# Latents and rotary key projected before the last two gated pairs, from unscaled products

## The chip, the cores and the metric

The kernel runs on one core of a Trainium2 chip. The metric is the device time of one execution in microseconds (us); the median of three runs of the kernel before is 1034.42 us. The engines are TensorE (PE; its weight loads appear as PEld), VectorE (DVE), ScalarE (ACT), GpSimd (POOL) and the queues that issue DMA transfers (SP for nearly all of them). Each engine works through a queue of its own in order; a wait at the head of a queue holds up everything behind it.

## The reference, cut to what matters

Two decoder layers over 512 tokens of 1024 channels, all in float32. Layer 0 normalises its input by rows (RMS norm) and multiplies it by one matrix `w_in`, whose 1696 columns are split:

```python
h = rmsnorm(x, norm_mix_e)                    # x / sqrt(mean(x^2) + EPS) * gain
proj = h @ w_in
a, g = proj[..., :512], proj[..., 512:1024]
u = a * sigmoid(g)                            # gated convolution branch
u = silu(layernorm(causal_dwconv(u, conv_w, conv_b)))   # 31 taps per channel
cq, ckv, kr = proj[..., 1024:1408], proj[..., 1408:1664], proj[..., 1664:]
q  = rmsnorm(cq, q_norm_g) @ w_uq             # 8 heads, 64 plain + 32 rotary columns
kv = rmsnorm(ckv, kv_norm_g) @ w_ukv          # keys and values of 8 heads
# causal attention, then concat([u, o]) @ w_out, residual; gated MLP
```

`cq` and `ckv` are the latents of the attention, `kr` is one rotary key that all heads share. Layer 1 is a pooling mixer and a second gated MLP. The change touches layer 0's mixer alone.

## The kernel before

Channels lie on the partitions and tokens along the free dimension, 512 to a tile. Every weight and every left operand is kept as the sum of two parts, `hi` and `lo`, and each 128x128x512 product is three matmuls (`mm3`, L107 to L109). A weight chunk arrives by DMA as `raw`, ACT copies it to `hi` (L96), DVE subtracts to get `lo` (L97), one chunk ahead of its use, in the order of the list `stream`.

The rows of `x` are multiplied by the norm's gain and projected before the norm's root is known. Its per-token factor `rows0` is applied to the products. `project` (L340s) makes one tile of 128 output columns: 24 matmuls from one `w_in` chunk. The first eight chunks carry four tiles at once (two gated pairs, `acc4`). `w_in1` has ten more chunks: four for the third and fourth gated pair, three for `cq`, two for `ckv`, one for the rotary key. They are projected in that order.

`glu` turns a pair of products into a tile `u` of the convolution: a product with `rows0`, a sigmoid on ACT, another product with `rows0`, one with the other half. Each `u` is convolved in the background. Some taps run on POOL (12, 12, 12 and 16 of the four tiles; L385 multiplies, L387 adds to `side`), one on ACT, the rest on DVE as multiply-adds into a PSUM tile `conv` (L367). A closing addition (L390) joins the two sums; the tiles' DVE taps follow one another. `pump(n, m)` puts the next n DVE taps and m POOL taps into the program.

`latent` projects `cq` or `ckv`: DVE multiplies the product by `rows0` into `t` (L447), ACT makes `hi` of `t` times the latent norm's gain (L101), DVE makes `lo` (L102), ACT squares `t` (L211) and DVE adds the squares (L213). After the key product, `rstd` sums the squares over channels on PE (L225), adds EPS (L229) and takes the inverse root in nine small DVE steps after two for the start value (L192 to L199). The result scales scores, values and keys; for the keys it is spread over partitions by four diagonals on DVE (L240) and products on PE (L241).

For each head, `scores` computes four row blocks. DVE adds the mask and takes the row maximum (L506), scales it by the query factor (L510), ACT takes the exponential (L514); a reciprocal (L520) and four ACT copies (L522) normalise. PE transposes one head behind (L536) and multiplies by the values two heads behind (L548). Queries (L492) are made two heads ahead, keys (L479) per pair of heads. The layer norm's transposes (L614) come when the last head and the convolution are done.

The framework fixes the order of each engine's queue when the program is built, from the traced program and estimates of its own, so instructions can stand in another order than in the code. `behind` keeps conv taps from filling in between the root's steps.

Of the kernel before, what the change touches and what calls it, by code (L numbers as in the profile page):

```python
# [44 lines left out]
def kernel(  # L45
# [71 lines left out]
    def rows_of(t, a, b):  # L117
        return t[a:b, 0, :], t[a:b, 1, :]

# [1 line left out]
    stream = (  # L121
        [(w_in0[k], 512) for k in range(KD)]
        + [(w_in1[m], 1024) for m in range(10)]
# [60 lines left out]
    held = []  # L184

    def behind(i):
        """Background work traced from here on starts after instruction i."""
        held[:] = [i]
# [14 lines left out]
    class Squares:  # L203
        """Sums of squares over the channels: tiles are added up, the last one apart."""
# [12 lines left out]
    def rstd(stats, blocks=range(4)):  # L217
        ps = aux()
        nb = len(blocks)
        v = small(nb * len(stats))  # L220
        for k, st in enumerate(stats):
            for i, b in enumerate(blocks):
                at = 2 * (nb * k + i)
                for n, t in enumerate(st.parts):
                    pe.matmul(  # L225
                        ps[:, at : at + 2], t[:, b * P : (b + 1) * P], ones[:, 0:2],
                        start=n == 0, stop=n == len(st.parts) - 1,
                    )
            dve.tensor_scalar(  # L229
                v[:, nb * k : nb * (k + 1)], ps[:, 2 * nb * k : 2 * nb * (k + 1) : 2],  # L230
                1.0 / st.n, EPS, op0=ALU.mult, op1=ALU.add,
            )
        return rsqrt(v, nb * len(stats))

    def spread_bank(r, blocks=2, tag="aux"):
        """Per-token column to rows: every partition gets the token's value."""
        ps = aux(tag)
        for i in range(blocks):
            d = p_t.tile([P, P], F32, tag="diag", bufs=4, name=uid("d"))
            dve.tensor_scalar(d, ident, r[:, i : i + 1], None, op0=ALU.mult)  # L240
            pe.matmul(ps[:, i * P : (i + 1) * P], ones, d, start=True, stop=True)  # L241
        return ps[:, : blocks * P]
# [7 lines left out]
    # ==== layer 0: conv + latent attention ====  # L250
# [22 lines left out]
    # rotary tables: the turn of each angle from exact products with the digits of 1/(2 pi)  # L273
# [54 lines left out]
    with tc.issue_after(opened.ins):  # L328
        for k in range(KD):
            stat.add(x[k])  # L330
    acc4 = [bank() for _ in range(4)]
    for k in range(KD):
        w = weights(2)
        for m in range(4):
            mm3(acc4[m], part(w, m), pair(xg[k]), k == 0, k == KD - 1)
        if k == 5:
            r0 = rstd([stat])
# [11 lines left out]
    # depthwise conv, in the background: taps on DVE into PSUM, the rest on ACT and Pool  # L349
# [61 lines left out]
    # GLU branch: u = a * sigmoid(g), kept behind CW - 1 zeros  # L411
# [19 lines left out]
    ps_a = project()  # L431
    pump(GLU, 2)
    ps_g = project()
    glu(ps_a, ps_g)
    pump(GLU, 2)
    ps_a = project()
    pump(GLU, 2)
    ps_g = project()
    glu(ps_a, ps_g)
    pump(GLU, 2)  # L440

    def latent(n, gain, width):
        parts, stat = [], Squares(width, dve)
        for m in range(n):
            ps = project()
            t = temp()
            dve.tensor_tensor(t, ps, rows0, op=ALU.mult)  # L447
            parts.append(s4())
            split_scaled(pair(parts[m]), t, c(gain + m))
            stat.add(t)  # L450
            pump(LAT, 2)
        return parts, stat
# [3 lines left out]
    # shared rotary key, replicated over the four row groups  # L456
# [4 lines left out]
    r = rstd([stat_q, stat_kv])  # L461
# [3 lines left out]
    pump(2, 2)  # L465
# [29 lines left out]
    def scores(h):  # L495
# [4 lines left out]
        for i in range(4):  # L500
# [9 lines left out]
            dve.scalar_tensor_tensor(  # L510
                nb[:, i : i + 1], mx[:, i : i + 1], -1.0, q_scale[:, i : i + 1],
                op0=ALU.mult, op1=ALU.mult,
            )
            act.activation(  # L514
                p, p, AF.Exp, bias=nb[:, i : i + 1],
                scale=q_scale[:, i : i + 1], accum_out=ls[:, i : i + 1],
            )
            blocks.append(p)
            pump(BLK, 1)
# [67 lines left out]
    # output projection: attention half first  # L587
# [20 lines left out]
    # layernorm over channels, token-major  # L608
# [42 lines left out]
    def residual(ps, m, gain, scale=None, apart=False):  # L651
        """x[m] += ps (scaled); its parts for the next product, and its squares."""
# [90 lines left out]
    def last_down(gs, ws):  # L743
        """The last channel tile by halves of the tokens, so that the final norm of the
        first half runs beside the products of the second."""
# [20 lines left out]
        def last_rstd():  # L766
            """The second half's columns, by a square root that one step refines."""
# [45 lines left out]
    # ==== layer 1: windowed means, as band matrices over tokens ====  # L813
# [62 lines left out]
def layout(inputs):  # L876
# [8 lines left out]
    def by_col(w):  # L885
        """[K, M] -> [M/128, 128, K/128, 128]: one stationary operand per column tile."""
# [54 lines left out]
    # constants of the shapes  # L941
# [51 lines left out]
```

## Time and profile before

| | |
|---|---|
| median of 3 runs | 1034.42 us (1031.65 to 1035.17) |
| span of the profiled execution | 1028.9 us, first to last instruction |
| busy in the span: PE, PEld, DVE | 989.6 us (96%), 795.5 us (77%), 607.6 us (59%) |
| busy in the span: ACT, POOL | 399.3 us (39%), 189.3 us (18%) |
| time of the profiled execution itself | not given beside the span; the median lies 5.5 us above the span |

Times in the profile count from the start of the span. A group row names line, engine, operation, tiles and shape, then the count, the busy time, the mean of one in ns, and the idle time ahead. A wait row reads: who waited for whom, us in total, times, longest. A queue row has start, duration and the instruction. "PEclk" or "granted clock" is the share of TensorE's full speed that it was given. A matmul's end is modelled, so a long row of matmuls overlaps in the listing.

### The profile page before, as it was taken

To read this page: it belongs to the slowest core of one execution; us is meant where nothing else is said; L and a number is where in the kernel's file an instruction comes from. 1 tells how busy PE (TensorE), PEld (TensorE's weight loads), DVE (VectorE), ACT (ScalarE), POOL (GpSimd) and SP (SyncE) were. 2 spreads that over 40 slices of the span, in tenths; PEclk is the share of its full clock that TensorE was granted. 3 is DMA by queue.
4 is the path that set the end of the run, shared out by engine and by line. 5 is a ranking of instruction groups with operands and counts; after the bars stand their busy time and mean duration, and the time that the engine had idled before them with its cause. 6 is when DMAs were issued, how large, how long until landed. Compare 5 with 4: busy or idle time off the path is not lost.

```text
span 1028.9 us, 11548 instructions
## 1 busy us (share of the span) xinstructions
PE 989.6 (96%) x4444; PEld 795.5 (77%) x4444; DVE 607.6 (59%) x901; ACT 399.3 (39%) x575; POOL 189.3 (18%) x191
## 2 busy tenths in 40 slices
PE   8996698999999999999999999999999999999996
PEld 6885465677888888888888889888888888888886
DVE  6989899958485556565432337585555655522223
ACT  5423277845253333333222235343333333322221
POOL 4399997004000000000001011300000000000101
PEclk9999699999999999999999999999999999999998
DMA  6422101013222222322222242222323222222212
GB/s 194 169 74 72 36 21 62 21 62 103 97 88 89 95 103 82 103 85 100 100 85 103 84 139 75 82 86 100 102 82 103 83 101 86 99 103 82 103 41 82
DMA packets 29479, 91.99 MB, mean 89 GB/s; under 512 B 4081, under 2 KB 6385, under 8 KB 29425
## 3 DMA queue, kind: packets, MB, share of 16 engines
q1 hardware_dynamic: 28880, 90.74, 25.8%
q8 instruction: 34, 0.56, 0.2%
q10 hardware_dynamic: 544, 0.52, 0.1%
q14 instruction: 21, 0.16, 0.1%
HBM read 89.02 MB, written 2.23 MB: 89 GB/s over the span
## 4 chain that ended last, share of the span: by engine, by line
PE 85%; DVE 11%; issue 1%; DMA 1%; ACT 1%; SPq 0%; DVEq 0%
PE ps L109 27%; PE ps L107 27%; PE ps L108 27%; DVE lo L97 2%; DVE conv L367 1%; DVE s L510 1%; DVE prob L506 1%; PE aux L225 1%; DVE xg L102 1%; PE ps L548 1%; PE aux L241 1%; DMA x<-in_xT_dram 0%; DMA col<-in_cols_dram 0%; DVE s L199 0%; DVE s L197 0%
## 5 line engine op out<-in xcount | busy, mean ns | idle before, releaser
L109 PE MATMUL ps<-xg,lo 128*128 128x512 f32 x816 | 323.8, 397 | 4.0 <-DVE lo L97 4.0
L107 PE MATMUL ps<-xg,hi 128*128 128x512 f32 x816 | 325.1, 398 | 2.0 <-ACT hi L96 2.0
L108 PE MATMUL ps<-xg,hi 128*128 128x512 f32 x816 | 324.2, 397 | 0.0
L96 ACT CAST hi<-raw 128x1024 fp32r<-128x1024 f32 (+2 forms) x166 | 169.6, 1024 | 393.3 <-PE ps L108 350.3
L97 DVE TENSOR_TENSOR lo<-raw,hi 128x1024 fp32r<-128x1024 f32 (+2 forms) x166 | 207.2, 1250 | 163.4 <-ACT hi L96 162.8
L109 PEld LDWEIGHTS ps<-xg,lo 128*128 128x128 f32 x816 | 154.0, 189 | 42.9 <-DVE lo L97 5.7
L107 PEld LDWEIGHTS ps<-xg,hi 128*128 128x128 f32 x816 | 154.3, 189 | 39.6 <-ACT hi L96 2.4
L108 PEld LDWEIGHTS ps<-xg,hi 128*128 128x128 f32 x816 | 154.3, 189 | 37.1
L107 PE MATMUL ps<-g,hi 128*128 128x512 f32 (+1 forms) x374 | 143.1, 383 | 0.0
L108 PE MATMUL ps<-g,hi 128*128 128x512 f32 (+1 forms) x374 | 142.9, 382 | 0.0
L109 PE MATMUL ps<-g,lo 128*128 128x512 f32 (+1 forms) x374 | 142.8, 382 | 0.0
L213 POOL TENSOR_TENSOR sqr<-sqr,sqr 128x512 f32<-128x512 f32 x33 | 51.3, 1553 | 322.7 <-ACT sqr L211 321.4
L688 POOL MEMSET t<- 128x2 f32 x44 | 4.3, 99 | 473.0 <-DVE t L702 362.4
L108 PEld LDWEIGHTS ps<-g,hi 128*128 128x128 f32 x374 | 70.4, 188 | 15.0
L107 PEld LDWEIGHTS ps<-g,hi 128*128 128x128 f32 x374 | 70.3, 188 | 15.0
L109 PEld LDWEIGHTS ps<-g,lo 128*128 128x128 f32 x374 | 70.3, 188 | 15.0
L689 DVE TENSOR_TENSOR t<-ps,rows 128x512 f32<-128x512 f32 x44 | 30.4, 690 | 83.8 <-PE ps L109 83.8
L701 DVE TENSOR_TENSOR t<-ps,rows 128x512 f32<-128x512 f32 x44 | 30.4, 690 | 75.0 <-PE ps L109 75.0
L387 POOL TENSOR_TENSOR side<-side,tapped 128x512 f32<-128x512 f32 x48 | 67.8, 1414 | 1.5
L696 DVE SCALAR_TENSOR_TENSOR t<-t,col,t 128x512 f32<-128x512 f32 x88 | 65.6, 748 | 1.4
L385 POOL TENSOR_TENSOR tapped<-u,col 128x512 f32<-128x512 f32 x48 | 59.8, 1267 | 0.0
L699 ACT ACTIVATE t<-t 128x512 f32<-128x512 f32 x44 | 27.8, 631 | 74.4 <-DVE t L696 74.4
(177 smaller groups left out, 935.4 us busy)
## 6 DMA issues: line engine op xcount, KB each, us to landing
raw<-in_w_up_dram SPq DMA_DIRECT2D x88, 512.0 KB, 3.2
raw<-in_w_down_dram SPq DMA_DIRECT2D x44, 512.0 KB, 3.3
raw<-in_w_in_dram SPq DMA_DIRECT2D x10, 512.0 KB, 3.3
raw<-in_w_out_dram SPq DMA_DIRECT2D x8, 512.0 KB, 3.3
x<-in_xT_dram SPq DMA_DIRECT2D x8, 256.0 KB, 4.3
raw<-in_w_in_dram SPq DMA_DIRECT2D x8, 256.0 KB, 3.6
raw<-in_w_uq_dram SPq DMA_DIRECT2D x4, 384.0 KB, 2.9
out_dram<-g SPq DMA_DIRECT2D x6, 256.0 KB, 2.3
```

Of the source, the lines that this page charges most:

```text
L96: i = act.copy(dst[0], src)
L97: dve.tensor_tensor(dst[1], src, dst[0].bitcast(F32), op=ALU.subtract)
L107: pe.matmul(ps, a[0], b[0], start=start, stop=False)
L108: pe.matmul(ps, a[0], b[1], start=False, stop=False)
L109: pe.matmul(ps, a[1], b[0], start=False, stop=stop)
L213: self.engine.tensor_tensor(self.parts[0], self.parts[0], t, op=ALU.add)
L385: pool.tensor_tensor(t, tap, w, op=ALU.mult)
L387: pool.tensor_tensor(side, side, t, op=ALU.add)
L689: dve.tensor_tensor(ut[:, 2 : 2 + S], pu, rows, op=ALU.mult)
L696: dve.scalar_tensor_tensor(a, ut[:, j : j + S], c(fw + j * NF + f), a, op0=ALU.mult, op1=ALU.add)
L699: act.activation(a, a, AF.Silu)
L701: dve.tensor_tensor(b, pv, rows, op=ALU.mult)
```

## The change

- The `stream` of weights takes chunks 4 to 9 of `w_in1` first, then 0 to 3. So the three `cq` tiles, two `ckv` tiles and the rotary key are projected right after the first two gated pairs, and the last two gated pairs (four tiles) after the latents' statistics have been issued.
- `latent` no longer multiplies by `rows0`. `lo` (L102), `hi` and the squares are taken from the product in PSUM. Since the latents' norms divide a token's factor out again, only EPS has to be adapted: the first `rstd` keeps `floor`, EPS times its mean square (with EPS), and the second adds `floor` in place of EPS.
- `pump(2, 2)` after the statistics goes; the pumps of the gated tiles move with them. The taps of POOL and DVE keep their numbers.
- In `scores` the scaled maximum is computed for two blocks at once, and their two exponentials follow it.

```diff
-        + [(w_in1[m], 1024) for m in range(10)]
+        + [(w_in1[m], 1024) for m in (4, 5, 6, 7, 8, 9, 0, 1, 2, 3)]
...
-    def rstd(stats, blocks=range(4)):
+    def rstd(stats, blocks=range(4), floor=None, keep=None):
...
+            if floor is None:
+                dve.tensor_scalar(vk, cols_of, 1.0 / st.n, EPS, op0=ALU.mult, op1=ALU.add)
+            else:
+                dve.scalar_tensor_tensor(
+                    vk, cols_of, 1.0 / st.n, floor, op0=ALU.mult, op1=ALU.add
+                )
+        if keep is not None:
+            dve.tensor_scalar(keep, v, EPS, None, op0=ALU.mult)
...
-            r0 = rstd([stat])
+            r0 = rstd([stat], keep=floor)
...
-    ps_a = project()
-    pump(GLU, 2)
-    ps_g = project()
-    glu(ps_a, ps_g)
-    pump(GLU, 2)
...
             ps = project()
-            t = temp()
-            dve.tensor_tensor(t, ps, rows0, op=ALU.mult)
             parts.append(s4())
-            split_scaled(pair(parts[m]), t, c(gain + m))
-            stat.add(t)
+            split_scaled(pair(parts[m]), ps, c(gain + m))
+            stat.add(ps)
             pump(LAT, 2)
...
-    r = rstd([stat_q, stat_kv])
+    r = rstd([stat_q, stat_kv], floor=floor)
...
-    pump(2, 2)
+    for _ in range(2):
+        ps_a = project()
+        pump(GLU, 2)
+        ps_g = project()
+        glu(ps_a, ps_g)
+        pump(GLU, 2)
...
-            dve.scalar_tensor_tensor(
-                nb[:, i : i + 1], mx[:, i : i + 1], -1.0, q_scale[:, i : i + 1],
-                op0=ALU.mult, op1=ALU.mult,
-            )
-            act.activation(
-                p, p, AF.Exp, bias=nb[:, i : i + 1],
-                scale=q_scale[:, i : i + 1], accum_out=ls[:, i : i + 1],
-            )
             blocks.append(p)
+            if i % 2:
+                two = slice(i - 1, i + 1)
+                dve.scalar_tensor_tensor(
+                    nb[:, two], mx[:, two], -1.0, q_scale[:, two], op0=ALU.mult, op1=ALU.mult
+                )
+                for n in (i - 1, i):
+                    act.activation(
+                        blocks[n], blocks[n], AF.Exp, bias=nb[:, n : n + 1],
+                        scale=q_scale[:, n : n + 1], accum_out=ls[:, n : n + 1],
+                    )
```

The queues, at three places. First DVE, one latent tile: before, the second `cq` tile.

```order
L447 TENSOR_TENSOR t_709<-ps_684,rows_389 128x512
L97 TENSOR_TENSOR lo_775<-raw_772,hi_774 128x1024
L102 SCALAR_TENSOR_TENSOR s_711<-t_709,col,s_711 128x512
L213 TENSOR_TENSOR sqr_667<-sqr_667,sqr_714 128x512
L367 SCALAR_TENSOR_TENSOR conv_818<-u_458,col,conv_818 128x512 x3
```

With the change, the same tile (lines are numbered anew: L376 is the tap that was L367).

```order
L102 SCALAR_TENSOR_TENSOR s_534<-ps_509,col,s_534 128x512
L376 SCALAR_TENSOR_TENSOR conv_498<-u_451,col,conv_498 128x512
L213 TENSOR_TENSOR sqr_492<-sqr_492,sqr_537 128x512
L376 SCALAR_TENSOR_TENSOR conv_498<-u_451,col,conv_498 128x512
L97 TENSOR_TENSOR lo_598<-raw_595,hi_597 128x1024
```

The product with `rows` is gone, and L102's first source is the PSUM tile `ps`. The taps here are the first channel tile's; counted up to head 0's first L506, DVE's queue holds 30 taps and one closing addition before, and 36 taps and two closing additions with the change.

Second PE, from the end of the key product on: before.

```order
L109 MATMUL ps_876<-xg_138,lo_825 128x512
L225 MATMUL aux_904<-sq,sqr_667 128x2 x4
L107 MATMUL ps_953<-s_664,hi_872 128x512
L108 MATMUL ps_953<-s_664,hi_872 128x512
L109 MATMUL ps_953<-s_664,lo_873 128x512
L107 MATMUL ps_953<-s_711,hi_872 128x512
L108 MATMUL ps_953<-s_711,hi_872 128x512
L225 MATMUL aux_904<-sq,sqr_808 128x2 x4
L109 MATMUL ps_953<-s_711,lo_873 128x512
```

With the change.

```order
L109 MATMUL ps_692<-xg_138,lo_643 128x512
L226 MATMUL aux_720<-sq,sqr_492 128x2 x4
L107 MATMUL ps_754<-xg_131,hi_688 128x512
L108 MATMUL ps_754<-xg_131,hi_688 128x512
L109 MATMUL ps_754<-xg_131,lo_689 128x512
L107 MATMUL ps_754<-xg_132,hi_688 128x512
L108 MATMUL ps_754<-xg_132,hi_688 128x512
L226 MATMUL aux_720<-sq,sqr_629 128x2 x4
L109 MATMUL ps_754<-xg_132,lo_689 128x512
```

Behind the two sums of squares (`aux`) stood head 0's query product, whose operands are the latents `s`; now the four gated tiles stand there, 96 matmuls on `xg`, and the queries follow them.

Third DVE, head 1's four score blocks: before.

```order
L506 ISA prob_1127,s_1128<-ps_1131,causal 128x128
L506 ISA s_1128 128x1
L506 ISA prob_1127,s_1128<-ps_1140,causal 128x256
L506 ISA s_1128 128x1
L510 SCALAR_TENSOR_TENSOR s_1129<-s_1128,q_scale 128x1
L506 ISA prob_1127,s_1128<-ps_1149,causal 128x384
L506 ISA s_1128 128x1
L510 SCALAR_TENSOR_TENSOR s_1129<-s_1128,q_scale 128x1
L367 SCALAR_TENSOR_TENSOR conv_818<-u_458,col,conv_818 128x512
L510 SCALAR_TENSOR_TENSOR s_1129<-s_1128,q_scale 128x1
```

With the change.

```order
L507 ISA prob_1111,s_1112<-ps_1115,causal 128x128
L507 ISA s_1112 128x1
L507 ISA prob_1111,s_1112<-ps_1122,causal 128x256
L507 ISA s_1112 128x1
L507 ISA prob_1111,s_1112<-ps_1130,causal 128x384
L507 ISA s_1112 128x1
L514 SCALAR_TENSOR_TENSOR s_1113<-s_1112,q_scale 128x2
L507 ISA prob_1111,s_1112<-ps_1137,causal 128x512
L507 ISA s_1112 128x1
L376 SCALAR_TENSOR_TENSOR conv_1303<-u_823,col,conv_1303 128x512
L514 SCALAR_TENSOR_TENSOR s_1113<-s_1112,q_scale 128x2
```

The scaling (L510, now L514) comes twice a head, two columns wide, and the first one stands behind the third block's maximum.

More of the change, by code (lines that the diff above doesn't have):

```diff
@@ L228, in rstd @@
                     )
-            dve.tensor_scalar(
-                v[:, nb * k : nb * (k + 1)], ps[:, 2 * nb * k : 2 * nb * (k + 1) : 2],
-                1.0 / st.n, EPS, op0=ALU.mult, op1=ALU.add,
-            )
+            cols_of = ps[:, 2 * nb * k : 2 * nb * (k + 1) : 2]
+            vk = v[:, nb * k : nb * (k + 1)]
+            if floor is None:
[6 more added lines that the diff above has]
+            dve.tensor_scalar(keep, v, EPS, None, op0=ALU.mult)
         return rsqrt(v, nb * len(stats))
@@ L330 @@
             stat.add(x[k])
+    floor = p_s.tile([P, 4], F32, tag="floor", bufs=1, name="floor")
     acc4 = [bank() for _ in range(4)]
@@ L430 @@
     glu(acc4[2], acc4[3])
-    ps_a = project()
-    pump(GLU, 2)
-    ps_g = project()
-    glu(ps_a, ps_g)
-    pump(GLU, 2)
[L436 to L440, printed above, removed]
     def latent(n, gain, width):
@@ L509, in scores @@
             )
-            dve.scalar_tensor_tensor(
-                nb[:, i : i + 1], mx[:, i : i + 1], -1.0, q_scale[:, i : i + 1],
-                op0=ALU.mult, op1=ALU.mult,
-            )
-            act.activation(
-                p, p, AF.Exp, bias=nb[:, i : i + 1],
-                scale=q_scale[:, i : i + 1], accum_out=ls[:, i : i + 1],
-            )
-            blocks.append(p)
+            blocks.append(p)
+            if i % 2:
[8 more added lines that the diff above has]
+                    )
             pump(BLK, 1)
```

## The prediction

> **What bounds the kernel now.** I read the waits of TensorE (PE) first, then the busy time by stretches, then VectorE's (DVE's) groups and its queue in order of time. Two waits of PE stand out between 60 and 235 us:
>
> ```profile
> PE aux L241 <- DVE d L240: 9.5, 1, 9.5
> PE aux L225 <- DVE s L229: 6.5, 1, 6.5
> DVE side L390 <- POOL side L387: 5.4, 1, 5.4
> DVE q L492 <- PE ps L109: 1.8, 1, 1.8
> DVE s L229 <- PE aux L225: 0.4, 1, 0.4
> ```
>
> PE stands twice, 6.5 and 9.5 us, both times for DVE: first for the latents' sums of squares, then for the diagonals that spread the key scale. The same stretches by engine (column: length, then busy time of PE, PEld, DVE, ACT, POOL, granted clock, DMA):
>
> ```profile
> 38.16:130.20 92.04, 74.03 (x310) 58.83 (x309) 82.22 (x91) 28.64 (x39) 87.26 (x65) 0.89 0.22 71
> 130.20:206.60 76.40, 70.00 (x312) 48.77 (x311) 73.40 (x170) 58.99 (x137) 42.24 (x36) 1.00 0.10 35
> 206.60:1028.90 822.30, 812.14 (x3666) 660.75 (x3664) 425.00 (x578) 290.37 (x366) 47.43 (x74) 1.00 0.27 92
> ```
>
> The first row runs from the first gated tile to head 0's first score reduction, the second from there to the layer norm's transposes, the third to the end. The change touches the first two; in the third PE works 812.14 of 822.30 us, and nothing there is altered, so it keeps its 822.30. In the second, DVE (73.40 of 76.40) is nearer to full than PE (70.00). In the first, DVE idles 9.8 us and PE 18. So DVE's queue sets both, and filling PE's hole only pays as far as DVE's queue becomes shorter. That is why I count DVE, not PE.
>
> What makes DVE slow is seen in its groups, by shape; 42 to 130 us:
>
> ```profile
> L367 DVE SCALAR_TENSOR_TENSOR conv<-u,col,conv 128x512 f32<-128x512 f32 x30 | 22.5, 750 | 0.6
> L102 DVE SCALAR_TENSOR_TENSOR s<-t,col,s 128x512 fp32r<-128x512 f32 x5 | 8.1, 1624 | 0.0
> L447 DVE TENSOR_TENSOR t<-ps,rows 128x512 f32<-128x512 f32 x5 | 3.4, 680 | 0.0
> L199 DVE SCALAR_TENSOR_TENSOR s<-s,s 128x8 f32<-128x8 f32 x3 | 3.4, 1122 | 0.1
> L197 DVE TENSOR_TENSOR s<-s 128x8 f32<-128x8 f32 x3 | 3.3, 1107 | 0.1
> ...
> L198 DVE SCALAR_TENSOR_TENSOR s<-s,s 128x8 f32<-128x8 f32 x3 | 2.4, 798 | 0.1
> ```
>
> and the score scaling in two stretches, 129.5 to 173 and 173 to 207 us:
>
> ```profile
> L510 DVE SCALAR_TENSOR_TENSOR s<-s,q_scale 128x1 f32<-128x1 f32 x20 | 13.6, 679 | 0.0
> ...
> L510 DVE SCALAR_TENSOR_TENSOR s<-s,q_scale 128x1 f32<-128x1 f32 x12 | 1.7, 148 | 0.0
> ```
>
> One column by another takes 148 ns late and 679 ns early. The difference is GpSimd (POOL), busy until about 173 us and idle after:
>
> ```profile
> 140.00:160.00 20.00, 17.75 (x81) 12.30 (x82) 19.89 (x47) 15.81 (x40) 19.68 (x18) 1.00 0.07 26
> 180.00:200.00 20.00, 19.02 (x86) 12.85 (x85) 19.04 (x50) 19.69 (x46) 0.00 (x0) 1.00 0.08 27
> ```
>
> Instructions with both tensors in SBUF (L102 from `t`, L197 to L199, L510) are long beside POOL; those with one tensor in PSUM (L367, L447) are not.
>
> **The change part by part.** In the first stretch, by difference on DVE. Durations overlap by some 0.08 us at a hand-over, so I use start-to-start times:
>
> ```profile
> 65.93 0.68 DVE L422 TENSOR_TENSOR u<-ps,t 128x512 f32<-128x512 f32 x1
> 66.53 0.68 DVE L447 TENSOR_TENSOR t<-ps,rows 128x512 f32<-128x512 f32 x1
> 67.13 1.83 DVE L97 TENSOR_TENSOR lo<-raw,hi 128x1024 fp32r<-128x1024 f32 x1
> 68.89 1.52 DVE L102 SCALAR_TENSOR_TENSOR s<-t,col,s 128x512 fp32r<-128x512 f32 x1
> 70.33 2.33 DVE L367 SCALAR_TENSOR_TENSOR conv<-u,col,conv 128x512 f32<-128x512 f32 x3
> ```
>
> 1. Five L447 go: 5 x 0.60 = 3.0 us less.
>
> 2. Five L102 now read PSUM. The trace has no such instruction. From above, nothing gained: they stay at 1.624 - 0.08 = 1.54 us. From below, L367's 0.750 - 0.08 = 0.67. I take 0.67, since L367 is the same operation with one operand in PSUM, beside the same POOL: 5 x 0.87 = 4.4 us less (0 to 4.4). A sentence on the page for this: the Trainium skill, "SBUF — State Buffer", "Who interferes with whom", says that a DVE instruction with two SBUF inputs contends with a GpSimd instruction that reads SBUF and one with at most one does not. By that rule the five are free, as taken; the trace agrees (680 ns beside 1624).
>
> 3. Idle time. The 5.4 us for POOL at the first channel tile's closing addition go: that addition now stands behind the root steps, some 10 us after POOL is done with the tile. The 1.8 us for the queries' product go too, as do the 0.4 us for the second statistic: 7.6 of the 9.8 us.
>
> 4. The new order puts 36 conv taps and two closing additions ahead of head 0's first score, where there are 30 and one now: 6 x 0.67 + 0.6 = 4.6 us more. They are not lost; they leave the second stretch.
>
> 5. The kept floor is one 128x4 operation ahead of the first norm's root, about 0.1 us (L510 alone is 0.148); the added operand of the second statistic reads PSUM and costs nothing. ACT's square and scaled copy now wait for PE instead of DVE; ACT is busy 28.64 of 92.04 us. No DMA is added. Weight chunks keep their places in SP's queue, only their contents change, so no transfer moves past another.
>
> Sum: 3.0 + 4.4 + 7.6 - 4.6 - 0.1 = 10.3 us. The first score reduction comes at 130.2 - 10.3 = 119.9 us.
>
> Does PE supply that? Its products come 0.23 us apart:
>
> ```profile
> 93.59 0.40 PE L108 MATMUL ps<-xg,hi 128*128 128x512 f32 x1
> 93.82 0.40 PE L109 MATMUL ps<-xg,lo 128*128 128x512 f32 x1
> ```
>
> A 24-product tile takes 5.6 us. Walking DVE's new queue from 38.2 us with the durations above, the key product leaves it at about 71 us, the nine root steps (3.4 + 3.3 + 2.4 us beside POOL and their hand-overs, as now) end at 83, the last `w_in` chunk is split at 89.5. PE has three gated tiles to do from 71 us (to 88), waits some 2 us for that chunk, and ends the fourth at 95: the root steps are covered by 17 us of products. If that cover were gone, they would cost PE 9.5 us again. What is late next is DVE's split of the query, key and value weights (96, 103 and 109 us): PE pauses some 1, 2 and 4 us there. The value products end at about 115, the keys leave DVE at 117, three taps and the second closing addition follow, then the score. PE has 4 us to spare.
>
> That second closing addition needs POOL to be done with the second channel tile, and the scores stand behind it in DVE's queue:
>
> ```profile
> 111.56 1.30 POOL L387 TENSOR_TENSOR side<-side,tapped 128x512 f32<-128x512 f32 x1
> 112.82 1.04 POOL L385 TENSOR_TENSOR side<-u,col 128x512 f32<-128x512 f32 x1
> ```
>
> POOL starts the third tile at 112.82 us now, 6 us ahead of DVE; with five fewer collisions it will not be later. Every us beyond 6 would cost one. The third and fourth gated tiles' inputs now leave DVE at some 99 and 112 us; POOL wants the third at 113 and the fourth twelve taps on, so this is hidden.
>
> In the second stretch DVE loses the 4.6 us, and half of the 32 score scalings. Beside POOL one costs 0.68 - 0.08 = 0.60, alone 0.07: now 20 x 0.60 + 12 x 0.07 = 12.8 us. Scores start 10.3 us sooner and POOL ends when it did, so some 13 pairs fall beside it: 13 x 0.60 + 3 x 0.07 = 8.0, 4.8 us less (from 0, were a pair to wait twice as long, to 6.4, half of all). DVE's busy 73.40 become 73.4 - 4.6 - 4.8 = 64.0. That is below PE's 70.00, so PE becomes the longest there, and what is gained is at most 76.4 - 70.0 = 6.4 us. PE's busy time contains drained ends, though (0.39 us for a product that the next follows after 0.23). Run back to back, its parts take less:
>
> ```profile
> 129.70 2.32 PE L503 MATMUL ps<-keys,q 128*128 128x128 f32 x8
> 193.50 3.46 PE ps L548 x14
> 201.15 1.09 PE ps L536 x10
> ```
>
> These are one head's scores, 14 pieces of values (8 a head) and one head's transposes: 8 x 2.3 + 7 x 2.0 + 8 x 1.1 us, with 54 products for queries, 18 for keys and 36 of the output projection at 0.23, make 66 us, a gain of 10. The other way, a head in which DVE still has more to do than PE (a weight split and a key pair beside its taps) holds PE up, and PE's lead in the next is not given back. I take 4.7 us, somewhat under the bound by busy time.
>
> All: 1028.9 - 10.3 - 4.7 = 1013.9 us span. The page gives no time of the profiled execution beside its span; the median of the three runs is 1034.42 - 1028.9 = 5.5 us above it, which I carry over: 1019.4 us.
>
> **The rivals.**
>
> *PE alone bounds the attention* (0.14). Queues run ahead enough that no head waits for DVE: 76.4 to 66 us, 10.4 instead of 4.7. For it: PE idles only 1 us in 180 to 200 us, where POOL is silent. Against: ACT is at 19.69 there, and is the next to be full. 1034.4 - 10.3 - 10.4 = 1013.7.
>
> *Waiting is not bought off* (0.12). The port behaves as a fixed loss of DVE's time: PSUM-fed L102 still block, pairs wait twice as long. First stretch 10.3 - 4.4 = 5.9, second 0: the hole in PE has only moved to where DVE still fills its row. 1028.5. Against it stand L447 and L367, which do not block.
>
> *The half clock* (0.09). PE's clock falls in its pauses:
>
> ```profile
> 98.00:100.00 2.00, 0.00 (x0) 0.00 (x0) 2.00 (x3) 1.57 (x3) 2.00 (x2) 0.56 0.25 101
> 106.00:108.00 2.00, 2.00 (x6) 1.56 (x5) 0.57 (x1) 0.00 (x0) 2.00 (x2) 0.50 0.54 197
> 106.11 0.43 PE ps L107
> 106.54 0.43 PE ps L108
> ```
>
> PE stops at 97; two us on the clock is down, and after the restart at 104 it is still at half, 0.43 us a product, into 108. The new pauses of 2 and 4 us ahead of the value products can do that too: 24 x 0.20 = 4.8 us, of which the 4 us to spare hide most; with head 0's start at half, some 3 us remain: 1022. The Trainium skill, "TensorE: Matmul & The Clock Gate", "Why this matters for your kernels", asks for no PE-idle gap over about 3 us; by that rule the last pause alone would do it; this trace has the drop after less than 3 us.
>
> *The pairs lengthen the chain* (0.05, the slower side). The first Exp of a head now waits for the second block's maximum, in the new order mostly for the third's too. In ACT's queue everything of that head stands behind it, and PE's transposes behind that:
>
> ```profile
> 165.12 0.41 DVE L506 CUSTOM_DVE_ANT_0 prob<-ps,causal 128x256 f32<-128x256 f32 x1
> 165.47 0.08 DVE L506 DVE_READ_ACCUMULATOR2_ANT s<- 128x1 f32 x1
> 165.47 0.43 DVE L510 SCALAR_TENSOR_TENSOR s<-s,q_scale 128x1 f32<-128x1 f32 x1
> 165.82 0.55 DVE L506 CUSTOM_DVE_ANT_0 prob<-ps,causal 128x384 f32<-128x384 f32 x1
> ```
>
> The delay is 0.35 to 0.35 + 0.48 = 0.83 us a head, up to 2.5 where a split stands between. Transposes lag their scores by a whole head, so I put it at 0. Exposed in full, 8 x 0.83 = 6.6 us; it decides from 15.0 / 8 = 1.9 us a head, and at 2.5 gives 1034.4 - 15.0 + 20 = 1039. For it: ACT is full late in the stretch and cannot catch up. Against: before 173 us DVE, not ACT, holds the heads up.
>
> **How the numbers follow.** The forecast, both gains near the sum, holds 0.60: 1019, with a range of its own of 1015 to 1024. The range reaches from just under PE's bound (1013.7) to just under the case without relief (1028.5): 1012 to 1027, which leaves out some 0.15. A change of 0.3%, 3.1 us, is about what a measurement of this kernel can tell from none. The forecast, PE's bound and the half clock are faster; of the 0.12 without relief 0.07 are faster, 0.04 within and 0.01 slower; of the pairs 0.01 is within and 0.04 slower. Faster 0.90, same 0.05, slower 0.05.
>
> **What would show it.** Right: L102 near 0.75 us; no wait of PE for the statistics or the diagonals; the first L507 near 120 us, 10 to 11 sooner; 16 score scalings at about 0.65 us beside POOL; the layer norm's transposes near 191 us. Wrong: L102 above 1.4 us; DVE waiting for POOL at the closing addition just ahead of the first score; a granted clock at half between 104 and 120 us with the score behind it; ACT idle ahead of the first Exp of most heads with PE waiting for its normalisation.

## The result, and the profile after

The changed kernel took 1018.74 us (median of four runs, 1016.27 to 1019.43) beside 1033.93 us for the kernel before in the same comparison: a ratio of 0.985, 95% interval 0.9833 to 0.9867, so 15 us faster. The span of the profiled execution is 1014.5 us.

The three stretches of the prediction after the change (length; busy time of PE, PEld, DVE, ACT, POOL; granted clock; DMA share and GB/s):

```profile
38.16:115.86 77.70, 73.94 (x316) 58.32 (x316) 73.92 (x93) 28.96 (x40) 73.41 (x55) 0.98 0.27 83
115.86:191.66 75.80, 69.02 (x304) 49.77 (x303) 65.62 (x148) 57.46 (x135) 55.17 (x46) 0.95 0.11 35
191.66:1014.50 822.84, 812.35 (x3666) 660.73 (x3664) 425.12 (x578) 290.35 (x366) 47.42 (x74) 1.00 0.28 91
```

The first stretch, from 38.16 us to head 0's first score reduction, went from 92.04 to 77.70 us: 14.3 us gained where 10.3 were forecast. The first gated tile began at 38.16 us before and begins at 37.67 now, so 0.5 us of this arose ahead of it. The second, to the layer norm's statistics, went from 76.40 to 75.80: 0.6 us where 4.7 were forecast. The third changed by 0.5 us. The total was forecast well; its two parts were not.

DVE's groups in the first stretch, by shape:

```profile
L97 DVE TENSOR_TENSOR lo<-raw,hi 128x1024 fp32r<-128x1024 f32 x9 | 13.4, 1490 | 0.3 <-ACT hi L96 0.3
...
L102 DVE SCALAR_TENSOR_TENSOR s<-ps,col,s 128x512 fp32r<-128x512 f32 x5 | 3.7, 745 | 0.2 <-ACT s L101 0.2
L213 DVE TENSOR_TENSOR sqr<-sqr,sqr 128x512 f32<-128x512 f32 x3 | 3.6, 1216 | 0.8 <-ACT sqr L211 0.7
...
L97 DVE TENSOR_TENSOR lo<-raw,hi 128x768 fp32r<-128x768 f32 x2 | 2.5, 1270 | 0.0
L199 DVE SCALAR_TENSOR_TENSOR s<-s,s 128x8 f32<-128x8 f32 x3 | 2.1, 695 | 0.1
```

L102 fell from 1624 to 745 ns, as forecast. Instructions that the change doesn't edit fell too. Before, in the same stretch:

```profile
L97 DVE TENSOR_TENSOR lo<-raw,hi 128x1024 fp32r<-128x1024 f32 x9 | 15.4, 1707 | 0.2 <-ACT hi L96 0.2
...
L213 DVE TENSOR_TENSOR sqr<-sqr,sqr 128x512 f32<-128x512 f32 x3 | 5.3, 1764 | 0.0
...
L97 DVE TENSOR_TENSOR lo<-raw,hi 128x768 fp32r<-128x768 f32 x2 | 4.1, 2034 | 0.0
```

The waits of PE and DVE, 60 to 235 us, with the change:

```profile
DVE bn L619 <- PE aux L617: 7.9, 2, 7.1
PE ps L539 <- ACT prob L525: 3.2, 2, 3.0
PE ps L107 <- DVE s L97: 2.1, 1, 2.1
PE ps L107 <- DVE t L423: 1.6, 1, 1.6
```

PE's 6.5 us for the statistics and 9.5 us for the diagonals are gone, and so is DVE's wait for POOL. A new wait heads the list, DVE's 7.1 us for the layer norm's transposes; it turned out to be the sign of what was missed.

### The profile page after: what moved, and what is told of

It reads as the page before. It is cut to its first block, busy times and chain, and to the rows that moved or that the text cites. A ratio compares the mean times of both kernels' runs of the same rounds, so it can differ in the third digit from the quotient of the medians.

```text
span 1014.5 us, 11528 instructions
## 1 busy us (share of the span) xinstructions
PE 987.5 (97%) x4444; PEld 794.3 (78%) x4444; DVE 592.3 (58%) x881; ACT 398.8 (39%) x575; POOL 188.5 (19%) x191
## 4 chain that ended last, share of the span: by engine, by line
PE 85%; DVE 10%; ACT 2%; issue 1%; DMA 1%; SPq 0%; DVEq 0%
PE ps L107 27%; PE ps L109 27%; PE ps L108 27%; DVE lo L97 2%; DVE conv L376 2%; PE ps L551 1%; DVE xg L102 1%; DVE prob L507 1%; PE aux L226 1%; DVE s L514 1%; ACT prob L525 1%; ACT prob L518 1%; PE ps L539 0%; PE aux L248 0%; DVE s L198 0%
## 5 line engine op out<-in xcount | busy, mean ns | idle before, releaser
L97 DVE TENSOR_TENSOR lo<-raw,hi 128x1024 fp32r<-128x1024 f32 (+2 forms) x166 | 205.5, 1240 | 164.3 <-ACT hi L96 164.3
L213 POOL TENSOR_TENSOR sqr<-sqr,sqr 128x512 f32<-128x512 f32 x33 | 51.4, 1557 | 322.1 <-ACT sqr L211 320.8
L394 POOL TENSOR_TENSOR tapped<-u,col 128x512 f32<-128x512 f32 x48 | 57.3, 1213 | 0.0
```

Source lines behind the costliest of these rows:

```text
L97: dve.tensor_tensor(dst[1], src, dst[0].bitcast(F32), op=ALU.subtract)
L213: self.engine.tensor_tensor(self.parts[0], self.parts[0], t, op=ALU.add)
L394: pool.tensor_tensor(t, tap, w, op=ALU.mult)
```

## The experiments

Each is an edit of the changed kernel, unless said otherwise. Times are medians beside the kernel before on the same chip.

### One part taken back at a time

**Pairs undone.** Each block's maximum is scaled alone, its exponential follows at once.

```diff
-            if i % 2:
-                two = slice(i - 1, i + 1)
-                dve.scalar_tensor_tensor(nb[:, two], mx[:, two], ...)
...
+            dve.scalar_tensor_tensor(nb[:, i : i + 1], mx[:, i : i + 1], ...)
+            act.activation(p, p, AF.Exp, ...)
```

> The changed kernel with the pairs undone: each score block's maximum is scaled alone and its exponential follows at once; order and unscaled latents stay. Theory of the prediction (a scaling costs DVE what it waits for POOL, 4.8 us in all): 16 scalings more at about 0.6 us beside POOL, DVE's busy time between the first score and the layer norm's transposes 65.6 -> about 72 us, the time 1 to 4 us over the changed kernel's 1018.7. Rival, the pairs lengthen the chain from maximum to transposes (3.0 us of PE's wait for head 0's normalisation): the time falls by 2 to 4 us. Rival, DVE no longer bounds the attention: within 1.5 us of 1018.7.

Measured: 1021.49 us, 2.8 slower than the change; ratio 0.9882 (0.9867 to 0.9897). First score at 116.41, second stretch 79.80 us with DVE at 72.23. The pairs are a gain, not a loss.

**Latents fed from SBUF.** ACT copies the unscaled product to SBUF, and L102 and the squares read the copy.

```diff
-            split_scaled(pair(parts[m]), ps, c(gain + m))
-            stat.add(ps)
+            t = temp()
+            act.copy(t, ps)
+            split_scaled(pair(parts[m]), t, c(gain + m))
+            stat.add(t)
```

> The changed kernel, but ACT copies each latent's product to SBUF first, and the lo part (L102), hi part and square are taken from that copy: DVE's count of instructions is the same, only L102 has both tensors in SBUF again. Theory of the port (a DVE instruction with both tensors in SBUF waits for the POOL instruction in progress, behind another such one for a whole one): L102 from 0.745 back to 1.4 to 1.7 us and the weight splits and square sums next to it longer by 0.2 to 0.5 us each as well; the first score from 115.9 to 121 to 125 us; time 1022 to 1027. Rival, each instruction pays for itself alone: L102 4 us more in all, neighbours unchanged, first score 120. Rival, the operand's place does not matter: 1018 to 1020.

Measured: 1020.54 us, ratio 0.987 (0.9855 to 0.9884); the ratio's interval overlaps the change's, so the time alone does not decide. First score at 119.26, 3.4 us later. DVE's groups in its first stretch:

```profile
L97 DVE TENSOR_TENSOR lo<-raw,hi 128x1024 fp32r<-128x1024 f32 x9 | 13.2, 1467 | 0.2 <-ACT hi L96 0.2
L102 DVE SCALAR_TENSOR_TENSOR s<-t,col,s 128x512 fp32r<-128x512 f32 x5 | 6.8, 1358 | 0.0
```

L102 is long again, 3.1 us in all. L213, whose own operands are in SBUF either way, takes 1523 ns instead of 1216; it now stands directly behind an L102 with both tensors in SBUF. L97 stays as short as with the change. So the source in PSUM shortens L102 and, through its place, L213, and the gain on L97 comes from elsewhere. The theory's figures (first score 121 to 125, 1022 to 1027 us) were missed; the rival in which each instruction pays for itself is nearer, but for L213.

**Order and pairs kept, latents scaled as before.** The product with `rows0` is back on DVE, and EPS stands in the second root as it did.

```diff
-            r0 = rstd([stat], keep=floor)
+            r0 = rstd([stat])
...
+            t = temp()
+            dve.tensor_tensor(t, ps, rows0, op=ALU.mult)
-            split_scaled(pair(parts[m]), ps, c(gain + m))
-            stat.add(ps)
+            split_scaled(pair(parts[m]), t, c(gain + m))
+            stat.add(t)
...
-    r = rstd([stat_q, stat_kv], floor=floor)
+    r = rstd([stat_q, stat_kv])
```

> The changed kernel with the latents scaled by rows0 as before (five products with rows0 on DVE, lo from SBUF), order and pairs of the change kept: what the unscaled latents are worth. Theory (DVE's queue bounds the first stretch): 3.0 us for the products, 4.4 for L102 and 2 to 4 for its neighbours, first score at 124 to 127 us, time 1026 to 1030. Rival, the order alone carries the gain since PE's two holes are filled either way: 1018 to 1022.

Measured: 1022.0 us, 3.3 slower than the change; ratio 0.989 (0.9872 to 0.9908). The first score comes at 124.45, 8.6 us later, but the layer norm only 4.4 us later (196.08): half of the delay is made good in the attention. The first score is in the theory's range (124 to 127), the time is not (1026 to 1030): it had left out what the attention gives back.

**Order of before, unscaled and pairs kept.**

```diff
-        + [(w_in1[m], 1024) for m in (4, 5, 6, 7, 8, 9, 0, 1, 2, 3)]
+        + [(w_in1[m], 1024) for m in range(10)]
...
+    for _ in range(2):      # the two gated pairs, ahead of the latents
...
-    for _ in range(2):      # the same, behind the statistics
...
+    pump(2, 2)
```

> The order of before (four gated tiles ahead of the latents, pump of two taps behind the root) with unscaled latents and pairs: what the order is worth. Theory (DVE's queue bounds): the shorter queue helps, but PE's wait for the diagonals stays at about 9 us and DVE's wait for POOL at the first closing addition stays or grows; first score at 120 to 125 us, time 1022 to 1027. Rival, the order carries all: 1031 to 1034. Rival, the order is worth nothing since DVE's row was full anyway: 1017 to 1020.

Measured: 1027.04 us, 8.3 slower than the change; ratio 0.9934 (0.9912 to 0.9955). Its first stretch, and the waits of 60 to 235 us:

```profile
37.81:125.47 87.66, 74.71 (x309) 59.75 (x309) 74.19 (x86) 28.31 (x39) 82.95 (x63) 0.90 0.23 74
```

```profile
PE aux L248 <- DVE d L247: 9.2, 2, 9.0
DVE side L399 <- POOL side L396: 6.5, 1, 6.5
...
PE aux L226 <- DVE s L235: 3.7, 1, 3.7
```

DVE's busy time fell from 82.22 to 74.19 us, 8.0 us, close to what the two edits of the latents take from it by durations (five L447, 3.4, and five L102, 8.1 - 3.7 = 4.4: 7.8). But DVE then idles 13.5 us instead of 9.8, and PE still waits for the statistics and the diagonals. The order is the largest of the three parts; without it the other two bring some 7 us. The first score, 125.47, and the time lie at the upper edge of what was expected.

### DVE beside POOL

**POOL nearly silent.** POOL keeps only the first tap of each channel tile.

```diff
-        pool_work.extend((lambda j=j: pool_tap(j)) for j in range(POOL_TAPS[m]))
+        pool_work.append(lambda: pool_tap(0))
```

> The changed kernel without POOL's convolution taps but the first of each channel tile (48 of 52 taps are left out of the sum, so the convolution is incomplete; DVE's taps are the same 68). Theory of the port: with POOL silent the root steps take 0.15 to 0.2 us each instead of about 1, weight splits of 1024 columns 1.22, the pair scalings 0.15; first score limited by PE's products to 106 to 108 us, the layer norm's transposes at 174 to 179, one run at 1001 to 1007. Rival, the lengths come from something else (operand shape, DVE's own queue): root steps stay near 1 us, the time within 3 us of 1018.7.

Measured: 999.14 us (one run), 2 us below the range; first score at 106.92, layer norm at 174.40, as expected. DVE's groups in its first stretch:

```profile
L247 DVE TENSOR_SCALAR d<-sq,s 128x128 f32<-128x128 f32 x4 | 1.0, 280 | 0.0
...
L197 DVE TENSOR_TENSOR s<-s 128x8 f32<-128x8 f32 x3 | 0.5, 168 | 0.1
L198 DVE SCALAR_TENSOR_TENSOR s<-s,s 128x8 f32<-128x8 f32 x3 | 0.5, 167 | 0.1
L199 DVE SCALAR_TENSOR_TENSOR s<-s,s 128x8 f32<-128x8 f32 x3 | 0.5, 167 | 0.1
```

The nine root steps take 1.5 us instead of 8.8. POOL is the cause of the long instructions, and it costs this kernel 20 us even after the change (less what the taps left out would themselves take elsewhere).

**A conv tap behind each root step.** `pump(1, 0)` after each of the nine steps, and `behind` no longer holds taps out of the root.

```diff
-    def rsqrt(v, n=4):
+    def rsqrt(v, n=4, fill=None):
...
+            if fill:
+                fill()          # after each of the three steps of a round
-        behind(last)
+        if not fill:
+            behind(last)
...
-    r = rstd([stat_q, stat_kv], floor=floor)
+    r = rstd([stat_q, stat_kv], floor=floor, fill=lambda: pump(1, 0))
```

> The changed kernel with one conv tap (PSUM operand) behind each step of the second root on DVE, instead of all taps held behind it. Theory of the port: a step waits for POOL's instruction in progress either way, so a 0.67 us tap ahead of it takes the place of the wait and is nearly free: the nine steps with nine taps take 11 to 14 us (9.4 without), the same taps later are saved; first score 2 to 5 us sooner than 115.9, time 1013 to 1018. Rival, each step waits as long as before and the tap comes on top: 15 to 16 us, first score unchanged or later, time 1018 to 1022.

Measured: 1020.53 us (1017.5 to 1021.48), ratio 0.9873 (0.9849 to 0.9897). DVE from the first root step to the last, 79.83 to 90.48 us:

```profile
L383 DVE SCALAR_TENSOR_TENSOR conv<-u,col,conv 128x512 f32<-128x512 f32 x8 | 5.9, 744 | 0.0
L197 DVE TENSOR_TENSOR s<-s 128x8 f32<-128x8 f32 x3 | 2.2, 739 | 0.0
L203 DVE SCALAR_TENSOR_TENSOR s<-s,s 128x8 f32<-128x8 f32 x3 | 1.9, 628 | 0.0
L200 DVE SCALAR_TENSOR_TENSOR s<-s,s 128x8 f32<-128x8 f32 x3 | 1.5, 502 | 0.0
```

With the change the nine steps alone, back to back, take 73.06 to 82.06 us:

```profile
L198 DVE SCALAR_TENSOR_TENSOR s<-s,s 128x8 f32<-128x8 f32 x3 | 3.4, 1131 | 0.1
L197 DVE TENSOR_TENSOR s<-s 128x8 f32<-128x8 f32 x3 | 3.3, 1108 | 0.1
L199 DVE SCALAR_TENSOR_TENSOR s<-s,s 128x8 f32<-128x8 f32 x3 | 2.1, 695 | 0.1
```

With eight taps among them, one split of 1.2 us and one product of 0.7, the steps take 10.65 us in all: the taps, 5.3 us elsewhere, are nearly free here. How long a small instruction lasts beside POOL depends on what stands ahead of it. Back to back, eight of the nine steps took 0.96 to 1.22 us, where POOL's instructions take 1.0 to 1.3. Behind a tap, which reads PSUM, they took less; that part of a wait for POOL is over by then is our reading of it.

The kernel didn't become faster: the first score came at 118.77, not sooner. With `behind` gone the edit did more than it meant to. 21 taps and the first closing addition, which waited 1.5 us for POOL, stand ahead of the first root step, where 15 taps and no closing addition stood; so the root ended at 90.48 us instead of 82.06.

### The second stretch

Why did it shorten by 0.6 us only, though DVE's work in it fell from 73.40 to 65.62? Cut at the end of DVE's last closing addition (L390, now L399), the windows show it. Before:

```profile
130.20:205.26 75.06, 68.66 (x305) 47.70 (x304) 73.40 (x169) 58.99 (x137) 42.24 (x36) 1.00 0.10 36
205.26:206.60 1.34, 1.34 (x9) 1.07 (x8) 0.01 (x2) 0.00 (x0) 0.00 (x0) 1.00 0.00 0
```

With the change:

```profile
115.86:183.14 67.28, 60.50 (x259) 42.68 (x258) 64.24 (x145) 54.15 (x130) 55.17 (x46) 0.95 0.12 40
183.14:191.66 8.52, 8.52 (x46) 7.09 (x45) 1.38 (x4) 3.31 (x6) 0.00 (x0) 1.00 0.00 0
```

Until its last closing addition DVE works 98% of the time before and 95% after. DVE's part became 7.8 us shorter. But PE still has 46 products to do then, 8.5 us, and DVE almost nothing: the two don't overlap there. Three experiments put this against other causes.

**The half clock.** 48 idle products of 128x128 keep PE working ahead of head 0's transposes.

```diff
+        if h == 0 and js == (0,):
+            for _ in range(48):
+                pe.matmul(ps[:, :P], idle, idle, start=True, stop=True)
```

> The changed kernel with 48 small products of a zero tile on PE ahead of head 0's transposes, in the 3.0 us in which PE waits for that head's normalisation; they are overwritten. Theory of the half clock (the granted clock of 0.95 in the second stretch costs it some 3 us, of which this pause about a third): the transposes and query products from 123.9 to 127.5 us run at full clock, 1.2 to 1.6 us sooner; time 1016.5 to 1018.7. Rival, the pause's clock is hidden behind DVE: no change, 1018 to 1019.5. If the products outlast the wait, they cost up to 1 us.

Measured: 1019.55 us, ratio 0.987 (0.9847 to 0.9892).

```profile
116.73:182.83 66.10, 59.99 (x299) 41.03 (x298) 65.11 (x144) 50.51 (x121) 56.06 (x46) 1.00 0.12 41
182.83:194.72 11.89, 11.89 (x58) 9.27 (x57) 1.56 (x4) 7.10 (x16) 0.00 (x0) 1.00 0.00 0
```

The granted clock is 1.00 instead of 0.95, and nothing is gained. But the edit doesn't rule the half clock out. The idle products ended at 125.97 us. ACT had begun to write the normalised blocks at 124.26, and with the change PE followed 0.46 us behind that; so the products outlasted the wait by some 1.2 us, about what the clock was expected to give. DVE's part became 1.2 us shorter, and PE has 58 products left behind it instead of 46. In the changed kernel there is also a second pause, behind which query products run at half clock, 0.43 us apart instead of 0.23, and DVE waits for the last of them:

```profile
163.90 0.63 PE L107 MATMUL ps<-s,hi 128*128 128x512 f32 x1
164.32 0.62 PE L108 MATMUL ps<-s,hi 128*128 128x512 f32 x1
```

```profile
165.22 0.69 DVE L493 TENSOR_TENSOR q<-ps,ctab 128x512 f32<-128x512 f32 x1 [0.84 <-PE ps L109]
```

What the clock can have cost in DVE's part is bounded by DVE's idle time there: 3.0 us with the change (67.28 - 64.24) and 1.0 here; with POOL silent in the next experiment it is 2.3, also at a clock of 1.00. PE's lone rest of 8.5 us ran at 1.00 in any case.

**POOL silent beside the attention alone.** The third and fourth channel tiles keep only POOL's first tap.

```diff
-        pool_work.extend((lambda j=j: pool_tap(j)) for j in range(POOL_TAPS[m]))
+        pool_work.extend((lambda j=j: pool_tap(j)) for j in range(POOL_TAPS[m] if m < 2 else 1))
```

> GpSimd does all its taps for the first two channel tiles, but only the first one of each for the third and fourth (26 of its 52 taps are left out), so that it is silent during the attention and as before until about 100 us. Theory: the second stretch is 4 us longer than forecast because the attention, started sooner, lies longer beside GpSimd. Then the first score stays near the changed kernel's 115.9 us (112 to 116, since its last 15 us are eased too), the second stretch takes 67 to 70 us as with GpSimd silent throughout (67.5), and the layer norm's statistics come at 180 to 185 us instead of 191.7. Rival: the second stretch is long for reasons of its own (the half clock, the order of the splits, two blocks behind one scaling): it stays at 73 to 76 us and the layer norm comes at 187 to 191 us.

Measured: 1009.25 us (one run); first score 117.25, second stretch 67.16 us, layer norm 184.41, inside what the theory expected but for the first score, 1.2 us above its bound. Its second stretch, cut in the same way:

```profile
117.25:175.82 58.57, 57.39 (x261) 40.84 (x260) 56.28 (x145) 52.98 (x130) 0.00 (x0) 1.00 0.13 46
175.82:184.41 8.59, 8.59 (x47) 7.14 (x46) 1.39 (x4) 3.38 (x6) 0.00 (x0) 1.00 0.00 0
```

DVE's busy time until the closing addition is 8.0 us less, and that part is 8.7 us shorter; PE's rest stays 8.6. So DVE's waits beside POOL are passed on in full. The paired scalings are most of them, 564 ns with the change and 152 here:

```profile
L514 DVE SCALAR_TENSOR_TENSOR s<-s,q_scale 128x2 f32<-128x2 f32 x16 | 9.0, 564 | 0.1
```

```profile
L514 DVE SCALAR_TENSOR_TENSOR s<-s,q_scale 128x2 f32<-128x2 f32 x16 | 2.4, 152 | 0.1
```

With these waits gone PE is busy for 57.39 of the 58.57 us, so there PE bounds that part as much as DVE does.

The kernel with scaled latents, which starts its attention 8.6 us later, fits: POOL lies beside its attention for 49.37 us instead of 55.17, DVE has 3.9 us less to do, and the same rest of PE follows.

```profile
124.45:187.50 63.05, 58.78 (x258) 41.41 (x257) 60.37 (x145) 53.71 (x130) 49.37 (x41) 0.97 0.13 42
187.50:196.08 8.58, 8.58 (x47) 7.12 (x46) 1.38 (x3) 3.38 (x6) 0.00 (x0) 1.00 0.00 0
```

POOL ends at 173 us before and at 172 with the change; a kernel that starts its attention sooner lies longer beside it.

**Head 0 without pairs.** In the changed kernel PE's longest stop in the attention is 3.0 us for head 0's normalisation. The queues of DVE, ACT and PE there:

```profile
117.56 1.39 DVE L97 TENSOR_TENSOR lo<-raw,hi 128x768 fp32r<-128x768 f32 x1
118.87 0.68 DVE L507 CUSTOM_DVE_ANT_0 prob<-ps,causal 128x512 f32<-128x512 f32 x1
...
119.48 0.75 DVE L376 SCALAR_TENSOR_TENSOR conv<-u,col,conv 128x512 f32<-128x512 f32 x1
120.14 0.95 DVE L514 SCALAR_TENSOR_TENSOR s<-s,q_scale 128x2 f32<-128x2 f32 x1
```

```profile
121.12 0.71 ACT L518 ACTIVATE prob<-prob,s,q_scale 128x384 f32<-128x384 f32 x1 [2.76 <-DVE s L514]
```

```profile
123.88 2.88 PE L539 MATMUL ps<-sq,prob 128*128 128x128 f32 x10 [3.00 <-ACT prob L525]
```

A weight split, a maximum, a tap and the scaling stand ahead of ACT's exponential: just what the slower rival of the prediction described, in one head.

```diff
-            if i % 2:
-                two = slice(i - 1, i + 1)
+            if h == 0 or i % 2:
+                two = slice(i - (h > 0), i + 1)
...
-                for n in (i - 1, i):
+                for n in range(i - (h > 0), i + 1):
```

> The changed kernel with the pairs undone for head 0 alone: there each block's maximum is scaled by itself and its exponential follows at once; heads 1 to 7 keep the pairs. In the changed kernel PE waits 3.0 us at 120.9 us for head 0's normalisation, because the scaling of its third and fourth block stands behind a weight split (1.39 us), a maximum and a conv tap. Theory: this stall is part of the 4 us that the second stretch misses, and the rest follows PE; then the stall is gone, the second stretch is 72 to 74 us instead of 75.8 and the time 1015.5 to 1017.5. Rival: the queue of DVE behind it is not shorter (two scalings more, 1.2 us), and what PE gains at head 0 it waits for at the next split: the stall is gone, the second stretch stays at 75 to 77 us and the time at 1018 to 1020.

Measured: 1018.88 us, ratio 0.9863 (0.9837 to 0.9888); second stretch 77.05 us. The stop is gone (PE's longest is now 1.7 us) and nothing is gained, as the rival expected: PE idles 7.4 us in the stretch, 6.8 with the change. Closing one stop opened others. DVE's part is 72.49 us here and PE's rest 4.56, so the place where DVE runs out moved too.

### Two faster versions

**Taps held behind the first score.** DVE idles 7 us at the end of the second stretch, while its queue sets when the first score comes. So the taps that are traced inside the attention may not move ahead of head 0's first score.

```diff
-            dve.tensor_tensor_reduce(
+            top = dve.tensor_tensor_reduce(
...
+            if h == 0 and i == 0:
+                behind(top)
```

> The changed kernel with the taps that are traced in the attention held behind head 0's first score maximum: 23 taps instead of 36 and one closing addition instead of two stand ahead of it on DVE. Theory (DVE bounds up to the first score, and has 7.1 us to spare ahead of the layer norm's transposes): first score 6 to 9 us sooner (107 to 110), the second stretch longer by 3 to 6 us, time 1013 to 1018. Rival, DVE and PE take turns in bounding the attention, and what is put there is paid in full: 1018 to 1021.

Measured: 1013.5 us (1012.83 to 1014.56), ratio 0.9811 (0.9792 to 0.9831): 5.2 us faster than the change by the medians, 4.0 by the ratios, with no work less. 23 taps and one closing addition stand ahead of the first score instead of 36 and two.

```profile
38.37:108.00 69.63, 69.57 (x310) 55.95 (x309) 65.92 (x79) 28.03 (x39) 65.00 (x47) 1.00 0.28 88
```

```profile
108.00:187.79 79.79, 74.19 (x320) 50.55 (x320) 76.51 (x160) 59.09 (x138) 64.46 (x54) 1.00 0.11 38
187.79:188.84 1.05, 1.05 (x8) 0.81 (x7) 0.70 (x3) 0.29 (x1) 0.00 (x0) 1.00 0.00 0
```

The first stretch is 8.1 us shorter than with the change, full of PE (69.57 of 69.63). The second is 5.0 longer, and PE's lone rest has shrunk from 8.5 to 1.05 us: DVE now has work to the end. The granted clock is 1.00 in both stretches, where it was 0.98 and 0.95; what share of the gain is the clock's was not separated.

**Both queue edits together.**

> Both edits that lie on DVE's queue together: one conv tap behind each step of the latents' root, and the taps that are traced inside the attention kept behind head 0's first score. 32 taps stand ahead of the first score instead of 36 (23 with the second edit alone, which took 1013.5 us). Theory: nine taps between the root's steps cost 1.5 us instead of the 6 us that they take elsewhere, and DVE is what fills the second stretch with the second edit alone (77.2 of 80.8 us), so the second stretch becomes 4 to 6 us shorter than its 80.8 while the first score comes 2 to 3 us later than its 108.0: 1010 to 1013 us. Rival: what is saved on DVE is lost again beside GpSimd or to PE in the attention, as it was with the root's taps alone: 1013 to 1018 us.

The edit is the sum of the two diffs. Measured: 1013.13 us (1011.87 to 1014.1), ratio 0.9789 (0.9773 to 0.9806), no different from the hold alone. The second stretch is 4.8 us shorter than with the hold alone (76.06), but the first score comes 5.5 us later (113.53). Of these, 2.4 us arise ahead of the first gated tile (40.77 instead of 38.37), which neither edit touches, and their reason was not found. The other 3.1 are close to the 2 to 3 expected; the closing addition waits 1.5 us for POOL, as with the root's taps alone.

## Why the prediction was right, and where it was not

The forecast of 1019 us and the direction were right. By steps:

- *Five products gone, five L102 from PSUM.* Right in size: 745 ns instead of 1624, as taken from L367. With the order of before, the two took 8.0 us of DVE's busy time where durations say 7.8. The Trainium skill, "SBUF — State Buffer", "Who interferes with whom", says that a DVE instruction with two SBUF inputs contends with a GpSimd instruction that reads SBUF, and that one with at most one, outside the two-port modes, does not. The trace agrees: 745 ns with an operand in PSUM, 1358 with both in SBUF.
- *Idle time, 7.6 of 9.8 us.* Nearly right: 3.8 us are left (77.70 - 73.92) instead of 2.2. The waits for POOL and for the queries' product went. The second statistic still cost 0.8 us, and the squares a new 0.7, now that ACT's square comes straight from PE.
- *Taps and closing addition moved ahead, 4.6 us; PE's supply; POOL in time.* Right: PE no longer waits for statistics or diagonals, the second closing addition did not wait, and POOL began the third tile at 104.72 us.
- *The sum of the first stretch, 10.3 us.* Too small by 4: the first score came at 115.86, not 119.9, and 0.5 of this is the earlier start. The missing term is the neighbours. L97 (2.0 and 1.6 us), L213 (1.7), L199 (1.3) and L428 (0.5) became shorter; L198 (1.0) and some small ones longer: some 5.3 us less on DVE in all, against 1.6 us more of idle time. The prediction kept the durations of every instruction that was not edited. For L97 of 1024 columns, the largest of them (1707 ns before, 1490 with the change), the latents' source is not the cause: with it in SBUF, L97 stayed at 1467 ns. With the order of before it takes 1641 ns and with the latents scaled 1558, so the larger part is the order. L213 goes the other way (1764 ns before, 1216 with the change): 1286 with the order of before, 1695 with the latents scaled. Which instruction ahead matters to which was not measured one by one.
- *DVE's work in the second stretch falls to 64.0 us.* Nearly right: 64.24 until its last closing addition, 65.62 in all.
- *"That is below PE's 70.00, so PE becomes the longest there."* This step failed. It compared two sums over the whole stretch, as if the engines could overlap to its end. They could in the kernel before, where DVE was full until 1.34 us ahead of the end. But the taps moved ahead and the shorter scalings leave DVE all but done 8.5 us before PE; up to then DVE is 95% busy and PE 90%. In five kernels with the changed order (the change, SBUF-fed, scaled, and the two with POOL quiet) that rest was 8.5 to 8.6 us, and ahead of it DVE was 94 to 96% busy; in the others of that order it was 1.05 to 12.3 us. 67.3 + 8.5 = 75.8 us. The prediction had priced the 4.6 us of moved taps as "not lost; they leave the second stretch"; they left it at its end, where DVE's time was worth nothing. The hold experiment puts 13 taps and a closing addition back behind the score and gains 4 to 5 us. How much of DVE's 3.0 us of idle time ahead of its last closing addition is due to PE's half clock stays open.
- *The rivals.* "PE alone bounds the attention" was wrong for the same reason; with POOL silent, PE's 66 us tally does come true (PE busy 65.98 of 67.16 us and, with POOL silent throughout, 67.30 of 67.48). "Waiting is not bought off" was wrong. The half clock did come, at 0.50 from 108 to 110 us ahead of the first score and at 0.95 over the second stretch. The first score was 4 us early all the same, and in the second stretch keeping the clock up gained nothing. The pairs did lengthen one head's chain by 3.0 us, but the pairs as a whole are worth 2.8 us, and undoing them there alone gained nothing.
- *From span to median* 5.5 us were carried over; it is 4.2 for the changed kernel. Its profiled execution took 1016.27 us, 1.8 above its span; the other 2.5 are that execution's distance from the median.

So the two errors, 4.0 us too little and 4.1 us too much, cancelled. That was luck.

Left open: what sets the work that PE is left with behind DVE's last closing addition. It is 12 us with a tap behind each root step and with the idle products, 6.6 with the pairs undone and 4.6 with head 0's alone undone, instead of 8.5.

## What to carry to other kernels

A stretch is bounded by the larger of two engines' sums only if both have work until its end: cut it where one of them runs out, and add what the other has left. Background work is worth keeping for the place where its engine would idle, not pulling ahead of a stage that waits for that engine; here moving 13 taps back was worth 4 to 5 us, beside the 15 of the whole change. Where two engines slow each other, as DVE and POOL do here, an instruction's length depends on its place in the queue, so a change of order reprices instructions that it doesn't edit.

## What the runs showed of the hardware

Not expected was how the wait of DVE beside POOL depends on the neighbour. Root steps of eight columns take 168 ns with POOL silent and 695 to 1131 ns back to back beside it; with a tap that reads PSUM between them they take 502 to 739 ns, so nine steps with eight taps, a split and a product took 10.65 us and nine steps alone 9.0. Four diagonals of 128x128 took 280 ns each with POOL silent and 837 beside it, and the scaling of a 128x4 tile by a constant (`q_scale`, one tensor in SBUF and none in PSUM) 162 and 609. TensorE was at half clock for some 7 us of the attention (granted clock 0.95 over 75.80 us). Keeping it at 1.00 with idle products gained no time, but these outlasted the wait by some 1.2 us, so that the half clock costs nothing is not shown.
